# A 4096 x 4096 x 4096 matmul with leaky ReLU in two levels of Winograd's seven products: one more product made of quarters, and the loads of b21 moved behind pieces of a22

## The chip, the cores and the metric

The kernel runs on one core of one Trainium2 chip. The metric is the device time of one execution in microseconds (us), as the median of the runs of a comparison. Before the change it is 1533.41 us, the median of three runs from 1532.85 to 1534.18.

## What is computed

```python
def setup_inputs():
    m, k, n = 4096, 4096, 4096
    return {"a": np.random.randn(m, k).astype(np.float32),
            "b": np.random.randn(k, n).astype(np.float32),
            "alpha": np.float32(0.01)}

def reference(a, b, alpha):
    x = np.matmul(a, b)
    return np.where(x > 0, x, alpha * x)
```

The kernel rounds both matrices to fp16, multiplies with fp32 sums, and applies the leaky ReLU to its fp32 results before they leave.

## The kernel before

**Regions.** The output is cut into 4 groups of 1024 rows (g = 0 to 3) and 4 strips of 1024 columns (j). The first region, (0, 0), is a stage of its own (lines 283 to 440). The other fifteen are made by one loop over `regions` (lines 505 and 506): (0,1), (0,2), (0,3), then (1,2), (1,0), (1,3), (1,1), the same order for g = 2, and (3,2), (3,0), (3,1), (3,3). The names below give a region as (g, j).

**Seven products.** A region is a 2 x 2 block product, made by Winograd's form with seven products in place of eight. `PRODUCTS` (line 653) lists them in their order: a11·b11, a12·b21, s2·b, s3·b, s1·b11', a22·b21', s4·b22', where the s are sums of blocks of A, made once for each group, and the primed blocks of B are sums that VectorE makes in place in every region. One product is 64 matmuls of 128x128 by 128x512 (`product`, line 809 within it). Numbers of products below count from one: the first, ..., the fifth (s1), the sixth (a22), the seventh (s4).

**Quarters.** In some regions the fourth, the sixth or the seventh product is itself made by seven quarter products (`quarter_product`, line 752 within it) of 16 matmuls of 128x128 by 128x256. Such a product has 112 matmuls, of half the width. It needs four more sums of its A block and four of its B block. The sums of A are made by VectorE once for a group (`sums_of_a`) and kept in DRAM (`kept_q`); SyncE loads them again for each region (`load_sums`), 512 KB each. The sums of B are made by VectorE in each region (`t3_of_b` in place, and `sums_of_b` into rooms of a 2 MB tile `t`). All regions with g > 0 other than the last of a group ("turning" regions) make the sixth and the seventh in quarters; all but the first of a group, from g = 1 on, make the fourth in quarters. The fifth is whole everywhere.

**What runs where.** TensorE makes the products in program order. VectorE makes sums, adds PSUM banks onto fp32 results (`add`, line 975; `more`, line 864; line 1133), turns the pieces of A (line 142, a stream transpose) and applies the leaky ReLU (line 313, in `leave`). ScalarE copies PSUM banks and squares data for a check of magnitudes. SyncE (SP) issues most loads and all stores of results; GpSimd (POOL) issues the loads that cast fp32 to fp16: A, and those blocks of B that are not kept. Each engine's queue is in program order. The order is written out by hand (`manual_schedule`), and a framework puts in the waits that buffers and PSUM banks need.

**The turning regions.** In (0,3), (1,1) and (2,1) the next group's A comes in, one 1024 x 1024 quadrant after the other, in four pieces of 512 KB each (`bring_a` = `fetch_a` on GpSimd, `turn_a_in` on VectorE). The last quadrant is a22. At the end of such a region stand, in program order: the loads of the next region's b11 (`fetch_b(i + 1, [(0, 0)], ks)`), the sixth product, then lines 1191 and 1192:

```python
        fetch_b(i + 1, [(1, 0)], (1, 0) if in_quarters else ks)
        bring_a(1, 1, range(3))
        leave(u2_pairs, 1, 0)
```

The first of these loads b21 (two halves of 1 MB, from SP, out of the fp16 copy `kept`), into the buffers that the sixth product reads. The next region's second product reads b21. The fourth piece of a22 comes after; then VectorE makes s1 and s2 of the new group, and in the next region its other sums.

**Other places that the prediction's steps touch.** Line 589 is `b_sum`, a sum of two B blocks. Lines 681, 687, 689 and 691 are the sums of B for quarters (the third, second, fourth and first in that order). Line 735 is in `sums_of_s3`, which makes the sums of s3 into rooms inside a22 and other blocks that are not read at that time; line 701 is in `sums_of_a`. Line 723 loads such a room again from DRAM, and line 770 is a tiny memset that a load of s2 waits for. Three `a16` buffers of 512 KB take the pieces of A and, in other parts, the quarter sums, and the squares of early checks of B (`EARLY`, lines 231 to 264).

Of the kernel before, what the change touches and what calls it, by code (L numbers as in the profile page):

```python
# [8 lines left out]
P = 128  # L9
# [15 lines left out]
KC = 8  # L25
# [6 lines left out]
MT = 4  # L32
# [16 lines left out]
def kernel(  # L49
# [469 lines left out]

    def fetch_unit(i, u, nt):  # L520
        g, j = regions[i]
        half = u // 2
        t = b_pool.tile([P, KC, NT], DT, name="b", tag=f"b{half + 1}{nt + 1}")
        have_b[i, u, nt] = t
        if g > 1 and j == CACHED and (half, nt) == (0, 1):
            move_t("t3", t, u, False)
        elif g and j == CACHED:
            nc.sync.dma_start(t, rows_of(kept[nt], u, 0, KC, True))
        elif half and (g and j == LAST or g > 1 and j in OTHERS):
            nc.sync.dma_start(t.rearrange("p c n -> p (c n)"), kept_half[j][u - 2, nt])  # L530
        else:
            for c in range(0, KC, 4):
                nc.gpsimd.dma_start(t[:, c:c + 4, :], b_rows(j, u, c, 4, nt, g > 0))  # L533
            if j == CACHED:
                wide = KC // (RUNS + [1, 1])[u]
                for c in range(0, KC, wide):
                    nc.sync.dma_start(rows_of(kept[nt], u, c, wide, False), t[:, c:c + wide, :])
# [122 lines left out]
    kept_s2 = dram_pool.tile([2, P, KC * RM], DT, name="kept_s2")  # L660
    kept_q = {name: dram_pool.tile([4, P, QUARTER], DT, name=f"kept_q{name}") for name in ("a22", "s4")}
    kept_s3 = dram_pool.tile([P, QUARTER], DT, name="kept_s3")
# [29 lines left out]

    def sums_of_a(g, name, room):

        x = {key: q.rearrange("p c m e -> p c (m e)") for key, q in quarters_of_a(g, name).items()}
        made = {}

        def make(n, x0, x1, op):
            made[n] = room(n)
            f = lambda t: made[t].rearrange("p (c m) -> p c m", m=2 * HALF) if isinstance(t, int) else x[t]  # L700
# [24 lines left out]
    def sums_of_s3(g, some, room=None):  # L725
# [4 lines left out]
        for n in some:  # L730
# [5 lines left out]
            if n == 4:  # L736
                nc.sync.dma_start(kept_s3, room)

    def s3_rooms(g):
# [43 lines left out]
    for i, (g, j) in enumerate(regions):  # L783
# [66 lines left out]

        def sixth_in_quarters(pairs, banks, v_pairs, v, y, tq, sq):

# [25 lines left out]
            quarter_product(x[0, 1], b[1, 0], into(fourth), True)  # L878
            leave(v_pairs, 1, 1)
            quarter_product(sx(2), t(2), into(one))  # L880
            following(2)
            more(0, 1, one)
            sums_of_b(y7, next_t, (2,))
            more(0, 0, fourth)
            quarter_product(sx(4), b[1, 1], into(other))
            following(1, sq[4])
            next_t[4] = tq[2]
            sums_of_b(y7, next_t, (4,))
            more(0, 1, other)
            quarter_product(sx(3), b[0, 1], into(one))  # L890
            following(3)
            more(1, 0, one)
            more(1, 1, one)
            quarter_product(x[1, 1], t(4), into(third), True)
            more(1, 0, third)
            next_t[1] = tq[4]
            sums_of_b(y7, next_t, (1,))
            return next_t, next_s

# [81 lines left out]

        def leave(pairs, h, nt):
            for r, t in enumerate(pairs):
                leaky(t.rearrange("p m n -> p (m n)"))
                for m in range(2):
# [41 lines left out]
        in_quarters = g > 0 and not turning  # L1027
        in_fourth = in_quarters and not first_of_group
        second_of_group = in_fourth and regions[i - 2][0] != g
        early = [measure(i, *block) for block in EARLY.get((g, j), [])]  # L1030
        for m in early[:1]:
            m.begin()
        if first_of_group and g:
            keep_s2(g)

        product(0, y, True)
# [82 lines left out]
        if late_ones:  # L1119
            late_ones[0].end()  # L1120
        if in_quarters and first_of_group:
            sq = {4: t[:, 3]}
# [4 lines left out]
        if in_fourth or turning and g:  # L1127
            v_pairs, v, parts = fourth_in_quarters(z, tq, {**s3_rooms(g), 4: a_quarter(sx4)})
            if turning:
                for n in range(3):  # L1130
                    turn_a_in(0, 1, n)
            for to, bank in parts:
                nc.vector.tensor_add(to, bank, to)
            if turning:
                add_v()
        else:
            product(3, z, True)
            v_pairs, v = keep(z, side)
        if in_fourth:
            sq = {n: t[:, 3] if n == 4 else new_a16() for n in (1, 2, 3, 4)}  # L1140
# [18 lines left out]
        if final:  # L1159
            judged = judge(b_pool.tile([1, P * 6], FP32, name="line", tag="b12"))  # L1160
            next(judged)
        if in_quarters:
            t3_of_b(quarters_of_b(i, 1, 0))
            sums_of_b(quarters_of_b(i, 1, 0), tq)
            t3_of_b(quarters_of_b(i, 1, 1))
            add_v()
            if final:
                good = next(judged)

        product(4, y, False)  # L1170
        if turning:
            new_s(g + 1, "s1")
        if in_quarters:
            tq, sq = sixth_in_quarters(u2_pairs, [new_bank(zbank + mt) for mt in range(MT)], v_pairs, v, y, tq, sq)
        else:
# [6 lines left out]
        if fifth:  # L1182
            fifth = measure(i + 1, *fifth)
            fifth.begin()
            fifth.end()
        fetch_b(i + 1, [(0, 0)], ks)

        if not in_quarters:
            product(5, z, g > 0)
            add(u2[::-1], z[::-1])  # L1190
        fetch_b(i + 1, [(1, 0)], (1, 0) if in_quarters else ks)
        bring_a(1, 1, range(3))
        leave(u2_pairs, 1, 0)
# [107 lines left out]
```

## Time and profile before

| what | value |
|---|---|
| median of 3 runs | 1533.41 us (1532.85 to 1534.18) |
| the profiled execution | 1537.09 us |
| its span, first to last instruction | 1535.2 us |
| TensorE busy | 1523.4 us, 8667 matmuls |
| VectorE busy | 1158.9 us, 1207 instructions |
| ScalarE busy | 425.5 us |
| granted TensorE clock, mean | 1.00 |
| moved by DMA | 351.26 MB, mean 229 GB/s |

The span is the time between the first and the last instruction of the profiled execution; what lies around it (1.9 us here) is not profiled. In the profile, idle time of an engine is put down to what ended it. A busy TensorE is counted from the start of a matmul to its modelled end, so a matmul's mean of 379 ns (128x512) is longer than the distance from one to the next, and lengths of products are better read from the distance of their starts.

Where the regions that matter begin, from the starts of their first matmuls: (0,3) 315.45 us, (1,2) 412.14, (1,0) 506.38, (2,2) 785.88, (2,0) 879.40, (2,3) 971.45, (2,1) 1063.38, (3,2) 1159.87, each with its products in the order above.

### The profile page before, as it was taken

What the parts mean: (1) busy time and instruction counts of PE and PEld (TensorE: products, weight loads), DVE (VectorE), ACT (ScalarE), POOL (GpSimd) and SP (SyncE); (2) the same over time, 40 slices, a digit from 0 to 9 for tenths busy, and PEclk for the clock granted to TensorE, in tenths of its full rate; (3) what the DMA queues carried; (4) which work ended last, traced back from release to release, by engine and by line L of the source; (5) the groups of instructions that cost most, each with busy time, mean ns of one, the idle gap of its engine ahead of it and who ended that gap; (6) DMA issues with size and microseconds to landing.
All of it is one profiled execution on the core that took longest, in us unless ns stands there. A gap on an engine that the chain in (4) does not pass through costs nothing. (4 is left out here: it accounts for less than half of the span.)

```text
span 1535.2 us, 21782 instructions
## 1 busy us (share of the span) xinstructions
PE 1523.4 (99%) x8667; PEld 846.8 (55%) x8667; DVE 1158.9 (75%) x1207; ACT 425.5 (28%) x730; POOL 258.3 (17%) x426
## 2 busy tenths in 40 slices
PE   9999999999999999999999999999999999999998
PEld 4444444444446567574544747557554475746656
DVE  4368867766699686768769798676987978687677
ACT  2201344646310213103551130312464103041210
POOL 5641110243202011022220001010331100101000
PEclk9999999999999999999999999999999999999999
DMA  9999895998879999899798939669899892949824
GB/s 246 183 212 209 232 280 174 177 195 177 223 284 280 252 288 272 249 288 259 168 284 272 319 147 207 268 154 323 168 228 298 230 345 75 292 160 193 306 97 140
DMA packets 192002, 351.26 MB, mean 229 GB/s; under 512 B 18705, under 2 KB 131601, under 8 KB 178834
## 3 DMA queue, kind: packets, MB, share of 16 engines
q0 software_dynamic: 119808, 112.22, 46.4%
q1 hardware_dynamic: 65458, 211.98, 37.1%
q10 hardware_dynamic: 6624, 25.56, 4.4%
q8 instruction: 70, 1.15, 0.3%
q14 instruction: 42, 0.34, 0.1%
HBM read 344.98 MB, written 114.82 MB: 300 GB/s over the span
## 5 line engine op out<-in xcount | busy, mean ns | idle before, releaser
L809 PE MATMUL ps<-b,a 128*128 128x512 f16 x2624 | 570.6, 379 | 0.0
L809 PE MATMUL ps<-b,s 128*128 128x512 f16 x2240 | 489.2, 379 | 0.4 <-DVE b L589 0.4
L809 PEld LDWEIGHTS <-a 128*128 128x128 f16 x2624 | 256.8, 98 | 307.6
L809 PEld LDWEIGHTS <-s 128*128 128x128 f16 x2240 | 219.1, 98 | 263.1 <-issue 1.2
L589 DVE TENSOR_TENSOR b<-b 128x4096 f16<-128x4096 f16 x104 | 234.7, 2287 | 47.1 <-DMA b<-in_b_dram 37.7
L533 POOL DMA_DIRECT2D b<-in_b_dram x128 | 94.9, 746 | 861.0 <-PE ps L752 436.8
L822 ACT COPY c<-ps 128x512 f32<-128x512 f32 x164 | 84.8, 596 | 468.1 <-PE ps L809 424.5
L142 DVE STREAM_TRANSPOSE a<-a 128x512 uint32<-128x512 uint32 (+2 forms) x120 | 127.2, 1108 | 100.8 <-DMA a<-in_a_dram 100.7
L133 POOL DMA_DIRECT2D a<-in_a_dram x252 | 137.5, 553 | 266.1 <-ACT junk L608 88.2
L752 PEld LDWEIGHTS <-q 128*128 128x128 f16 x1424 | 139.3, 98 | 16.8 <-issue 0.7
L608 ACT ACTIVATE junk<-a 128x512 bf16<-128x512 f16 x192 | 121.1, 631 | 98.6 <-DMA a<-in_a_dram 93.2
L313 DVE SCALAR_TENSOR_TENSOR c<-c 128x1024 f32<-128x1024 f32 (+2 forms) x123 | 141.7, 1194 | 3.4 <-ACT c L822 3.2
L231 ACT ACTIVATE sq<-b 128x2048 bf16<-128x2048 f16 x64 | 118.4, 1910 | 38.7 <-DVE sq L240 30.9
L975 DVE TENSOR_TENSOR c<-ps,c 128x512 f32<-128x512 f32 x140 | 87.5, 682 | 55.0 <-PE ps L809 41.7
L752 PEld LDWEIGHTS <-a 128*128 128x128 f16 x1200 | 117.4, 98 | 19.0 <-issue 1.4
L283 PE MATMUL ps<-b,a 128*128 128x512 f16 x512 | 112.5, 379 | 1.6 <-DVE a L142 1.0
L752 PE MATMUL ps<-b,q 128*128 128x256 f16 x784 | 92.0, 273 | 0.6 <-DVE c L864 0.6
L752 PE MATMUL ps<-b,a 128*128 128x256 f16 x752 | 88.3, 273 | 0.0
L283 PEld LDWEIGHTS <-a 128*128 128x128 f16 x512 | 49.6, 98 | 62.4 <-issue 1.8
L911 ACT COPY c<-ps 128x512 f32<-128x512 f32 x9 | 5.3, 587 | 269.8 <-DMA out_dram<-c 118.9
L752 PEld LDWEIGHTS <-s 128*128 128x128 f16 x624 | 61.1, 98 | 7.1
L864 DVE TENSOR_TENSOR c<-ps,c 128x512 f32<-128x512 f32 x80 | 52.3, 687 | 14.3 <-PE ps L752 14.3
(104 smaller groups left out, 904.1 us busy)
## 6 DMA issues: line engine op xcount, KB each, us to landing
b<-in_b_dram POOLq DMA_DIRECT2D x136, 512.0 KB, 11.7
out_dram<-c SPq DMA_DIRECT2D x240, 256.0 KB, 6.4
a<-in_a_dram POOLq DMA_DIRECT2D x244, 128.0 KB, 5.7
b<-kept_half SPq DMA_DIRECT2D x28, 1024.0 KB, 11.1
b<-kept SPq DMA_DIRECT2D x20, 1024.0 KB, 9.2
q<-kept_qs ACTq DMA_DIRECT2D x40, 512.0 KB, 7.7
s<-kept_s SPq DMA_DIRECT2D x18, 1024.0 KB, 7.7
q<-kept_qa SPq DMA_DIRECT2D x28, 512.0 KB, 7.8
```

Source lines behind the costliest of these rows:

```text
L133: nc.gpsimd.dma_start(a16[32 * q:32 * q + 32], src.rearrange("(g i) w -> i g w", i=32))
L142: nc.vector.transpose(part.rearrange("p c m e -> p c (m e)").bitcast(U32) .rearrange("p c (g i) -> p g c i", i=32), src[:, :, i * n:(i + 1 ...
L231: nc.scalar.activation(to, self.parts[n], SQUARE)
L283: nc.tensor.matmul(ps, a_cols(at[0, h, u], c, mt, (h, u) == (0, 0)), bt[0, u, nt][:, c, :], start=first, stop=last,)
L313: nc.vector.scalar_tensor_tensor(t, t, alpha, t, op0=MULT, op1=MAX if alpha <= 1 else MIN)
L533: nc.gpsimd.dma_start(t[:, c:c + 4, :], b_rows(j, u, c, 4, nt, g > 0))
L589: nc.vector.tensor_tensor(f(to), f(x0), f(x1), op)
L608: nc.scalar.activation(junk, piece[:, q, :], SQUARE, accum_out=to[:, 4 * n + q:4 * n + q + 1])
L752: nc.tensor.matmul(to[m], xq[:, c // 2, rows, c % 2], yq[:, c, :], start=first and c == 0 and m < banks, stop=c == KC - 1, skip_group_chec ...
L809: nc.tensor.matmul(banks[mt], a_cols(t, c, mt, t is first_a), B(half, nt, k)[:, c, :], start=first and (k, c) == todo[0], stop=(k, c) == t ...
L822: nc.scalar.copy(kept[mt], banks[mt])
L975: nc.vector.tensor_add(to, bank, to)
```

## The change

It does two things.

**b21 behind a22.** In turning regions, b21's first half is loaded after the second piece of a22 is turned, and its second half after the third. A memset of one column on VectorE stands before each load and writes its buffer, so that the load, on SP, waits for VectorE to come to it. The halves come in the order 0, 1.

**The fifth in quarters in (2,3).** A new function makes it. For it, (2,0) makes the four sums of s1 and keeps them in DRAM, and (2,3) loads them. Its partial sums go from PSUM by ScalarE into rooms in a22 (where a sum of s3 lay), and from there VectorE adds them onto the banks `y`. So that sum of s3 is kept in DRAM too (in (2,2)), and loaded again at the start of (2,1). The sums of B for the sixth, which were made during the fifth, are now made between the steps of the fifth and the sixth, and the sums of A for the sixth are loaded after those of the fifth.

```diff
-    def fetch_unit(i, u, nt):
+    def fetch_unit(i, u, nt, later=False):
         t = b_pool.tile([P, KC, NT], DT, name="b", tag=f"b{half + 1}{nt + 1}")
         have_b[i, u, nt] = t
+        if later:
+            nc.vector.memset(t[:, :1, :1], 0.0)
...
+    FIFTH = {(2, 3)}
+    kept_s31 = dram_pool.tile([P, QUARTER], DT, name="kept_s31")
...
             nc.vector.tensor_tensor(sx[n], x0, x1, op)
             if n == 4:
                 nc.sync.dma_start(kept_s3, room)
+            if n == 1 and g in [of for of, _ in FIFTH]:
+                nc.sync.dma_start(by_chunk(kept_s31), sx[1])
...
+        def fifth_in_quarters(y, one, other, tq, sq, between):
+            b = quarters_of_b(i, 0, 0)
+            x = quarters_of_a(g, "s1")
+            t = lambda n: b_quarter(tq[n])
+            sx = lambda n: a_quarter(sq[n])
+            onto = lambda r, n: [y[2 * r + m][:, n * HALF:(n + 1) * HALF] for m in range(2)]
+            rooms = by_chunk(x21(g, "a22")).bitcast(FP32)
+            rooms = [rooms[:, :2], rooms[:, 2:]]
+            def copied(bank):
+                rooms.append(rooms.pop(0))
+                nc.scalar.copy(rooms[1], pair(bank))
+                return rooms[1]
+            def more(r, n, room):
+                for m, to in enumerate(onto(r, n)):
+                    nc.vector.tensor_add(to, to, room[:, m])
+            quarter_product(x[0, 0], b[0, 0], into(one), True)
+            room = copied(one)
+            quarter_product(sx(4), b[1, 1], onto(0, 1))
+            more(0, 0, room)
+            next(between)
+            quarter_product(x[1, 1], t(4), onto(1, 0))
+            quarter_product(sx(2), t(2), into(one))
+            room = copied(one)
+            quarter_product(x[0, 1], b[1, 0], onto(0, 0))
+            more(0, 1, room)
+            next(between)
+            quarter_product(sx(1), t(1), into(other), True)
+            room = copied(other)
+            more(0, 1, room)
+            more(1, 1, room)
+            quarter_product(sx(3), b[0, 1], into(one))
+            room = copied(one)
+            for m in range(2):
+                to = pair(y[2 + m])
+                nc.vector.tensor_add(to, to, room[:, m].unsqueeze(1).to_broadcast([P, 2, HALF]))
...
-            leave(v_pairs, 1, 1)
+            if between:
+                next(between)
+            else:
+                leave(v_pairs, 1, 1)
             quarter_product(sx(2), t(2), into(one))
             following(2)
             more(0, 1, one)
+            if between:
+                t3_of_b(y7)
             sums_of_b(y7, next_t, (2,))
             more(0, 0, fourth)
+            if between:
+                leave(v_pairs, 1, 1, (0,))
...
             sums_of_b(y7, next_t, (1,))
+            if between:
+                leave(v_pairs, 1, 1, (1,))
...
+        if i and regions[i - 1] in FIFTH:
+            for c in range(KC // 2):
+                nc.sync.dma_start(by_chunk(x21(g, "a22"))[:, c], by_chunk(kept_s31)[:, c])
         product(0, y, True)
...
+        s1_sums = {}
+        if s1_here:
+            sums_of_a(g, "s1", lambda n: t[:, n - 1], (1, 2, 3), s1_sums)
+        if in_fifth:
+            t5 = {2: t[:, 0], 4: t[:, 1], 1: t[:, 2]}
+            t3_of_b(quarters_of_b(i, 0, 0))
+            sums_of_b(quarters_of_b(i, 0, 0), t5, (2, 4))
...
-            for to, bank in parts:
+            for n, (to, bank) in enumerate(parts):
+                if in_fifth and n == 2:
+                    sums_of_b(quarters_of_b(i, 0, 0), t5, (1,))
                 nc.vector.tensor_add(to, bank, to)
-            if turning:
+            if turning or in_fifth:
                 add_v()
...
-        if in_fourth:
+        if s1_here:
+            sums_of_a(g, "s1", lambda n: t[:, 3], (4,), s1_sums)
+        if in_fifth:
+            s5 = {n: t[:, 3] if n == 3 else new_a16() for n in (4, 2, 1, 3)}
+            load_sums("s1", s5, (4, 2, 1, 3))
+        elif in_fourth:
...
+        if in_fifth:
+            fifth_in_quarters(y, new_bank(zbank + 3), new_bank(zbank + 1), t5, s5, between)
+            sq = {n: t[:, 3] if n == 3 else new_a16() for n in (1, 2, 4, 3)}
+            load_sums("a22", sq, (1, 2, 4, 3))
...
-        fetch_b(i + 1, [(1, 0)], (1, 0) if in_quarters else ks)
-        bring_a(1, 1, range(3))
+        if turning:
+            bring_a(1, 1, [0, 1])
+            fetch_unit(i + 1, 2, 0, True)
+            bring_a(1, 1, [2])
+            fetch_unit(i + 1, 3, 0, True)
+        else:
+            fetch_b(i + 1, [(1, 0)], (1, 0) if in_quarters else ks)
         leave(u2_pairs, 1, 0)
```

`for_the_sixth` is the generator that `between` stands for: it makes the sums of B for the sixth in three steps, one at each `next`. In the sixth of (2,3) the rooms and banks are taken in another order, so that none waits for the fifth's last steps.

## Prediction

> **What bounds the kernel now.** I read the page's head first, then TensorE's waits, then the chain of waits in order of time, and then VectorE's timeline ahead of each wait found.
>
> ```profile
> PE 1523.4 (99%) x8667; PEld 846.8 (55%) x8667; DVE 1158.9 (75%) x1207; ACT 425.5 (28%) x730; POOL 258.3 (17%) x426
> ...
> PE ps L752 <- DVE q L689: 1.2, 1, 1.2
> ...
> PE ps L752 <- DVE c L864: 0.6, 1, 0.6
> PE ps L809 <- DVE b L589: 0.4, 1, 0.4
> ```
>
> TensorE is busy for 99% of the span at clock 1.00. Only three waits lie after the first region. So there are two ways to gain: fewer columns through TensorE, and these three waits. From the starts of the matmuls around them they cost more than the rows' idle time: (1,2)'s sixth takes 12.95 us instead of 12.23 (0.73 lost), (1,0)'s second product 14.34 instead of 13.81 (0.53), (2,1)'s fourth 13.61 instead of 12.23 (1.39). The chain prices a product:
>
> ```profile
> 1107.17 1.24 DVE q L687
> 1108.40 0.02 issue
> 1108.42 1.24 DVE q L689
> 1109.66 0.04 issue
> 1109.70 8.89 PE ps L752 x80
> ...
> 1295.00 12.23 PE ps L752 x112
> 1307.22 13.81 PE ps L809 x64
> ```
>
> A product in quarters takes 12.23 us, a whole one 13.81. Everything after 1109.70 is TensorE without a gap, so whatever is won or lost by then reaches the end undiminished. Next, VectorE where A comes in at the end of (0,3), and in (1,0):
>
> ```profile
> 409.91 2.11 DVE L142 STREAM_TRANSPOSE a<-a 128x512 uint32<-128x512 uint32 x2 [8.89 <-DMA a<-in_a_dram]
> ...
> 489.92 0.69 DVE L864 TENSOR_TENSOR c<-ps,c 128x512 f32<-128x512 f32 x1
> ...
> 529.71 2.29 DVE L589 TENSOR_TENSOR b<-b 128x4096 f16<-128x4096 f16 x1 [8.86 <-DMA b<-in_b_dram]
> ...
> 534.77 4.62 DVE L589 TENSOR_TENSOR b<-b 128x4096 f16<-128x4096 f16 x2 [0.39 <-DMA b<-in_b_dram]
> ```
>
> VectorE sits idle for 8.89 us until a22's first piece is there. From then to 463 us it has nearly no idle time, and at 489.92 it gives a bank free 0.73 us late: it carries its lateness from the turn. The wait in (1,0) comes from loads of b: from 461 to 535 us the DMA engines are full in each slice (mean share 1.13), and the 16 loads of b there take a median of 24.4 us. The third place is (2,1):
>
> ```profile
> 1018.00:1046.00 28.00, 28.00 (x196) 18.98 (x195) 20.36 (x22) 1.76 (x3) 5.91 (x8) 1.00 1.10 220
> 1046.00:1074.00 28.00, 28.00 (x211) 20.41 (x210) 19.06 (x23) 9.84 (x9) 0.00 (x0) 1.00 1.00 373
> 1074.00:1078.00 4.00, 4.00 (x20) 1.82 (x19) 3.81 (x8) 1.62 (x4) 2.54 (x5) 1.00 0.49 97
> 1078.00:1093.00 15.00, 15.00 (x72) 6.77 (x70) 12.01 (x10) 5.68 (x16) 6.12 (x12) 1.00 1.06 194
> ...
> 1090.38 2.11 DVE L142 STREAM_TRANSPOSE a<-a 128x512 uint32<-128x512 uint32 x2 [2.49 <-DMA a<-in_a_dram]
> 1092.82 2.10 DVE L142 STREAM_TRANSPOSE a<-a 128x512 uint32<-128x512 uint32 x2 [0.33 <-DMA a<-in_a_dram]
> ```
>
> The last two columns of the windows are DMA share and GB/s: full from 1018 to 1074, half idle for 4 us, full again. VectorE waits for pieces of A until 1092.82 and then works without a gap to the sum (L689) that TensorE takes at 1109.70. So (2,1)'s wait is one of arriving data.
>
> **The change part by part.** *b21 behind a22, at (0,3).* b11 and b21 (4 MB) now stand ahead of the pieces; 2 MB of it go behind. The transfers from 391 to 410 run at the rate of 1 MB in about 3.3 us, so the pieces come some 6 us earlier, and with them VectorE's sums for (1,2). A few of these will then meet other limits (b22 lands at about 427, where VectorE takes it at 432.34 now), so I count 5 us. That is more than 0.73: the wait in (1,2) goes, -0.73. VectorE's stores (kept_s, kept_q) go out 5 us sooner too, partly into DMA time that is idle around 452, ahead of the full stretch of 461 to 535; its end, the last b22, then moves from 534.7 to some time between 530 and 534.7. The wait there is 0.53, and TensorE comes there 0.73 earlier, so the wait goes if that end moves by 1.3 us or more, of some 4.5 possible: -0.53. Sum -1.26; bounds 0 and -1.26. On the other side stands b21 itself: first half issued at about 407, second at 410, and the 1 MB loads of this kind land in a median of 9.2 us (12.4 us where pieces come beside them), so at 419 to 422; the second product takes it at 425.95 and 432.9. Covered by 7 us. VectorE's memsets are of 0.06 us (the one on L770), and their buffers are free by then: the sixth product ends at 398.3. Queued behind the waiting load on SP are only u2's stores, which VectorE makes ready later still; queued behind the memsets on VectorE is the third piece, which isn't there yet. At (1,1) and (2,1) the same move gains nothing, since (2,2) and (3,2) have no wait.
>
> *The fifth in quarters.* 13.81 - 12.23 = -1.58. Its start waits for VectorE: after the sums of B at 1020.83 it now makes three sums for quarters (1.25, 1.25, 1.14) before it frees bank `fourth` (0.69), at 1025.2 against a start at 1025.11: +0.1. Then come two adds, one sum (1.14), three adds, `add_v` (2.35) and the first adds of 128x256 onto `y`. No row has an add from PSUM to PSUM; the nearest, L940, takes 0.43 into SBUF, so 0.9 for two, done at 1031.8. TensorE needs them at 1032.2: 0.4 in hand. At twice the price it would wait 0.5; below nothing it can't cost. The rest of VectorE's work fits into its 3.68 us of idle time ahead of 1038.48 and, spread, into the sixth.
>
> *Loads of sums in (2,3).* The four for the fifth go where those for the sixth went, issued 1018.3 to 1023.6, the last landed by 1032.8, needed at 1035.6. Those for the sixth now go when buffers come free, at 1028.7, 1032.2, 1035.7 and 1037.4, and are needed at 1039.2, 1042.7, 1044.4 and 1046.2. Rows for such loads here: median 8.9 us on SP, 7.4 to 10.4 on ACT's queue 10 us later. So the margins are 1.6, 1.6, -0.2 and -0.1: I take +0.3 of new wait, bounds 0 and 1.7.
>
> The Trainium skill bears on this: DMA: Bandwidth & Descriptors (Queues, rings and completion order) says each DMA engine takes turns between queues by packet. From 1018.5 to 1046 SP's queue moved 2.10 MB in 576 packets and GpSimd's 4.05 MB in 4071, 3.6 KB and 1.0 KB each; by that rule the sums would win over b's loads and come without a wait, which makes 1531.2. But the loads of 1018 to 1024 took 8.9 us all the same, so the sum goes by the row.
>
> *Sums of s1 in (2,0).* Four on VectorE, 4 x 1.22 = 4.9 us, beside idle time of 3.68 + 1.11 + 0.69 there. Their rooms in `t` are wanted again: VectorE must wait until the stores (issued at about 932 to 934.3) have landed. Stores of this kind took 6.6 to 7.4 us in (1,2) at equal load, so 942: VectorE goes on with the sum that TensorE wants at 948.7 ready at 945. SP's loads for the sixth wait behind the fourth store, issued at about 938.4 instead of 926.4; the last needs that store landed (946), lands at 953.5 and is needed at 954. I take +0.2, bounds 0 and 3.5 (landings of 13.3 us, as kept_half's stores).
>
> *(2,1).* The fifth brings 2 MB more, and the kept s3 sum 0.5 MB: at 373 GB/s 6.7 us of DMA inside the full stretch. Against it are 2 us idle after 1074, and pieces that GpSimd can issue 1.5 us sooner, as TensorE is earlier. With s2's 1 MB load standing amid the pieces in either case, I expect them about 1.2 us sooner on the clock where TensorE is 1.5 us sooner, so the wait grows by 0.3: +0.3. Bounds: -1.39 (wait gone) and 6.7 - 2.0 = 4.7 later on the clock, which is +6.2 against a TensorE that is 1.5 earlier.
>
> Sum: -1.26 - 1.58 + 0.1 + 0.3 + 0.2 + 0.3 = -1.94. The profiled execution took 1537.09 (span 1535.2), 3.7 above the median; I take the sum off the median: 1533.41 - 1.94 = **1531.5 us**.
>
> **The rivals.** (A) *Pieces of (2,1) late, slower than before.* The backlog of 6.7 us is met by only 2 us of idle DMA, so the last piece lands 4.7 us later, the chain to L689 shifts whole, and the fifth's gain drowns in the wait: -1.26 + 4.7 = +3.4, 1536.9. For it: shares of 1.00 to 1.10 over 56 us. Against it: most of the extra bytes come early, and GpSimd's loads of b11 and b12, landed by 1052.5 and used from 1063 on, can give way. It decides from a landing 1.3 us later on.
>
> (B) *The wait of (2,1) goes as well.* Pieces come with TensorE's earlier start and v's stores, now split and later, leave room: -1.26 - 1.58 + 0.1 - 1.39 = -4.1, 1529.3. Against it: nothing in the change brings these pieces forward.
>
> (C) *b21's move doesn't do what it says*: VectorE's lead is lost to waits for stores of sums (it has such waits of 0.5 to 0.8 at 463 to 474), and both waits of group 1 stay: -0.68, 1532.7. For it: the DMA engines are full there. Against: 5 us of lead for 0.73.
>
> (D) *(2,0) waits for its stores*: +3.5 in place of 0.2: 1534.8. For it: b's loads beside them take 10.5 us. Against: 6.6 to 7.4 for the same stores.
>
> **How the numbers follow.** Forecast 0.52, A 0.08, B 0.17, C 0.12, D 0.11. The forecast's own spread is 1530.3 to 1533. Less than 0.2% (3.07 us: below 1530.34, above 1536.48) I take as about what a measurement can't tell from no change. Faster: B and 0.03 of the forecast, 0.20. Slower: A and 0.02 of D, 0.10. Same: 0.70. The range 1529.4 to 1534.9 leaves out A and about half of B.
>
> **What would show it.** Right: no wait on L864 in (1,2) and none on L589 in (1,0); VectorE's idle time at the end of (0,3) down from 8.89 to about 3; the fifth of (2,3) in 12.2 to 12.5 us; a wait of 1 to 3.5 us on L689's successor in (2,1). Wrong: TensorE waiting in (2,0)'s sixth for a sum or its load, more than 1 us in (2,3)'s sixth, a second product in (1,2), (2,2) or (3,2) that waits for b21, or (2,1)'s fourth above 16 us.

## The result, and the profile after

The changed kernel takes 1537.74 us, the median of 11 executions from 1534.06 to 1543.66. The kernel before, in the same comparison, takes 1534.02 (11 executions, 1532.54 to 1536.68). The ratio is 1.0024, 95% interval 1.0014 to 1.0034: 3.72 us slower, just over the 3.07 us below which the prediction takes two times as the same. The forecast was 1531.5, the range 1529.4 to 1534.9; the result lies outside it.

The profiled execution of after took 1537.21 us (span 1534.3), that of before 1537.09 (span 1535.2). So the two profiles end together, though the medians are 3.7 apart. That has to be understood first, and it is done by cutting a profile into the stretch from the start of region (0,1) to the modelled end of the last matmul, which holds everything that was changed, and the rest, which holds the first region and what lies around the span:

| profile | execution us | (0,1) starts | stretch us | rest us |
|---|---|---|---|---|
| before | 1537.09 | 122.06 | 1407.30 | 129.79 |
| after | 1537.21 | 120.57 | 1408.58 | 128.63 |
| after, five more executions | 1537.12, 1535.69, 1535.95, 1534.90, 1536.39 | 120.69 to 121.32 | 1407.59, 1406.65, 1406.24, 1405.48, 1407.24 | 129.04 to 129.71 |
| s31_alone (below): nothing in the stretch waits | 1532.31 | 120.51 | 1404.66 | 127.65 |

The rest is 127.65 to 130.77 us in the twenty profiles of this study. In the six profiles of kernels whose fifth is whole it is 128.42 on average, in the six of after 129.25. Before's median of 1534.02 less 128.42 is 1405.6, so the usual execution of before loses some 0.9 us to waits in the stretch (at most 1.7, by the smallest rest), where its profile lost 2.65. This is an estimate, since before was profiled once, and that profile was taken on an execution above all eleven others. After's median less 129.25 is 1408.5. So of the 3.7 us between the medians some 2.9 lie in the stretch and some 0.8 outside it.

The part outside can be seen without a profile too, since the span of every execution is on record. What lies around the span is 1.87 to 2.17 us in all 106 executions of before that the experiments were compared with, and 1.96 to 3.07 us in the eleven of after, with a median of 2.93. Behind the span the trace has no instruction of the program, but it has loads of instructions (8 KB each): one in before's profile, which ends 2.1 us behind the span, and two in after's, the second ending 3.2 us behind it. That this second load takes the time is likely and not shown. The prediction has no term for it.

TensorE's waits after (the line, what it waited for, us in total, times, longest):

```profile
PE ps L762 <- DVE q L694: 2.8, 1, 2.8
...
PE ps L762 <- ACT c L977: 1.1, 1, 1.1
PE ps L819 <- DMA b<-in_b_dram: 0.8, 1, 0.8
```

L762, L819, L694 and L592 are L752, L809, L689 and L589 of before. The two waits of group 1 are gone, and of the three above, two are new. The lengths of the products, from one start to the next, where they are not the full 13.81 (whole) or 12.23 us (quarters) in each profile ((2,0)'s second product, 13.93, and the last product of all, 12.39, are left out, being the same in before):

| product | before | after | five more executions of after |
|---|---|---|---|
| (1,2) sixth | 12.95 | 12.23 | 12.23 each |
| (1,0) second | 14.34 | 13.81 | 13.81 each |
| (2,0) sixth | 12.23 | 12.36 | 13.22, 12.56, 12.41, 13.12, 13.22 |
| (2,3) first | 13.81 | 14.79 | 13.81 each |
| (2,3) fourth | 12.23 | 12.47 | 12.46 or 12.47 |
| (2,3) fifth | 13.81 | 12.22 | 12.22 each |
| (2,3) seventh | 12.23 | 13.45 | 13.47, 13.41, 13.43, 13.47, 13.47 |
| (2,1) fourth | 13.61 | 15.17 | 14.27, 14.06, 13.78, 12.28, 13.92 |

After's column against before's sums to +1.29, which is the difference of the two stretches (1.28): nothing is lost anywhere else. Now the places in turn.

*b21 behind a22.* VectorE at the end of (0,3) (start, us, line, operation, and in brackets the idle time and what ended it):

```profile
401.46 2.10 DVE L142 STREAM_TRANSPOSE a<-a 128x512 uint32<-128x512 uint32 x2 [1.94 <-DMA a<-in_a_dram]
404.19 2.11 DVE L142 STREAM_TRANSPOSE a<-a 128x512 uint32<-128x512 uint32 x2 [0.63 <-DMA a<-in_a_dram]
```

The idle time of 8.89 us ahead of a22 is 1.94 now, and the first piece is turned 8.5 us sooner (7.0 sooner counted from the start of (0,1)).

*The fifth.* VectorE's adds from SBUF onto PSUM, which no row of before had, and the seventh's place on ScalarE:

```profile
1029.38 0.76 DVE L881 TENSOR_TENSOR ps<-ps,a 128x256 f32<-128x256 f32 x2
...
1032.62 0.76 DVE L881 TENSOR_TENSOR ps<-ps,a 128x256 f32<-128x256 f32 x2 [1.35 <-PE ps L762]
...
1046.74 1.22 DVE L313 SCALAR_TENSOR_TENSOR c<-c 128x1024 f32<-128x1024 f32 x1
```
```profile
1055.75 0.59 ACT L977 COPY c<-ps 128x512 f32<-128x512 f32 x1 [18.97 <-DMA out_dram<-c]
```

A pair of adds takes 0.76, overlap included, and VectorE is there 1.35 us ahead of TensorE for the second pair. But v's first pair of output blocks now gets its leaky ReLU only at 1046.74 (L313), its stores are issued at 1047.98, and the seventh's first copy (L977) needs one of those `c` buffers: it waits for the store until 1055.75, and TensorE waits for the copy. Before, v left as a whole, earlier in the sixth.

*(2,1).* VectorE where the pieces of A come in, and the chain behind it:

```profile
1084.08 2.11 DVE L142 STREAM_TRANSPOSE a<-a 128x512 uint32<-128x512 uint32 x2
1090.05 2.10 DVE L142 STREAM_TRANSPOSE a<-a 128x512 uint32<-128x512 uint32 x2 [3.86 <-DMA a<-in_a_dram]
1092.62 2.11 DVE L142 STREAM_TRANSPOSE a<-a 128x512 uint32<-128x512 uint32 x2 [0.47 <-DMA a<-in_a_dram]
```
```profile
1108.22 1.24 DVE q L694
1109.46 0.04 issue
1109.50 8.89 PE ps L762 x80
```

The last sum comes at 1109.46 where it came at 1109.66; counted from the start of (0,1) that is 1.29 us later, while TensorE wants it 0.27 sooner (its start in the fourth, 1103.06 against 1104.82 by the same count). The DMA engines in the windows shown of before (the last two columns: DMA share, GB/s):

```profile
1046.00:1074.00 28.00, 26.94 (x192) 18.57 (x190) 21.39 (x27) 10.64 (x10) 0.55 (x1) 1.00 1.06 366
1074.00:1078.00 4.00, 4.00 (x20) 1.79 (x19) 3.89 (x7) 1.07 (x2) 3.75 (x7) 1.00 1.09 308
```

The 4 us that were half idle (share 0.49) are full now (1.09). The execution moves 356.50 MB in place of 351.26: the sums of s1 are stored and loaded (4.2 MB), the kept s3 sum too (1.0 MB). Who pays is seen in the landings from 1013 to 1046, first before, then after:

```profile
b<-in_b_dram POOLq DMA_DIRECT2D x8, 512.0 KB, 9.9
q<-kept_qa SPq DMA_DIRECT2D x4, 512.0 KB, 8.9
```
```profile
b<-in_b_dram POOLq DMA_DIRECT2D x8, 512.0 KB, 13.0
q<-kept_qs SPq DMA_DIRECT2D x4, 512.0 KB, 7.7
q<-kept_qa SPq DMA_DIRECT2D x4, 512.0 KB, 6.5
```

There are twice the loads of sums on SP, and both groups land sooner, in the median, than the one did before; GpSimd's casting loads go from 9.9 to 13.0 us. The pieces of A in (2,1) are GpSimd's loads too: the first of them took 2.8 us from its issue to its landing before (issued at 1074.46), and takes 6.4 us after (issued at 1072.69). The rule of the Trainium skill that the prediction weighed (DMA: Bandwidth & Descriptors, Queues, rings and completion order: turns by packet) agrees with this pair of rows.

### The profile page after: what moved, and what is told of

The parts are those of the page before. It is cut to its first block, busy times and chain, and to the rows that moved or that the text cites. A ratio compares the mean times of both kernels' runs of the same rounds, so it can differ in the third digit from the quotient of the medians.

```text
span 1534.3 us, 21931 instructions
## 1 busy us (share of the span) xinstructions
PE 1522.1 (99%) x8715; PEld 851.6 (56%) x8715; DVE 1172.4 (76%) x1231; ACT 428.2 (28%) x734; POOL 258.8 (17%) x426
## 2 busy tenths in 40 slices
DMA packets 194258, 356.50 MB, mean 232 GB/s; under 512 B 18913, under 2 KB 132833, under 8 KB 181090
## 5 line engine op out<-in xcount | busy, mean ns | idle before, releaser
L819 PE MATMUL ps<-b,a 128*128 128x512 f16 x2624 | 570.7, 379 | 0.8 <-DMA b<-in_b_dram 0.8
L819 PE MATMUL ps<-b,s 128*128 128x512 f16 x2176 | 475.2, 379 | 0.0
L819 PEld LDWEIGHTS <-a 128*128 128x128 f16 x2624 | 256.7, 98 | 308.7 <-issue 1.1
L819 PEld LDWEIGHTS <-s 128*128 128x128 f16 x2176 | 212.9, 98 | 255.2 <-issue 0.4
L592 DVE TENSOR_TENSOR b<-b 128x4096 f16<-128x4096 f16 x104 | 234.7, 2286 | 45.6 <-DMA b<-in_b_dram 30.7
L762 PEld LDWEIGHTS <-q 128*128 128x128 f16 x1488 | 145.5, 98 | 18.3 <-issue 1.2
L313 DVE SCALAR_TENSOR_TENSOR c<-c 128x1024 f32<-128x1024 f32 (+2 forms) x123 | 141.8, 1192 | 3.7 <-ACT c L832 3.5
L762 PEld LDWEIGHTS <-a 128*128 128x128 f16 x1200 | 117.4, 98 | 20.4 <-issue 3.0
L1041 DVE TENSOR_TENSOR c<-ps,c 128x512 f32<-128x512 f32 x140 | 87.6, 683 | 44.7 <-PE ps L819 33.5
L762 PE MATMUL ps<-b,q 128*128 128x256 f16 x816 | 95.6, 273 | 0.0
L762 PE MATMUL ps<-b,a 128*128 128x256 f16 x752 | 88.3, 273 | 0.0
L977 ACT COPY c<-ps 128x512 f32<-128x512 f32 x9 | 5.3, 586 | 256.9 <-PE ps L762 122.9
L762 PEld LDWEIGHTS <-s 128*128 128x128 f16 x672 | 65.8, 98 | 7.8 <-issue 0.2
L762 PE MATMUL ps<-q,q 128*128 128x256 f16 x528 | 62.9, 273 | 1.1 <-ACT c L977 1.1
```

What stands on the lines that cost most here:

```text
L313: nc.vector.scalar_tensor_tensor(t, t, alpha, t, op0=MULT, op1=MAX if alpha <= 1 else MIN)
L592: nc.vector.tensor_tensor(f(to), f(x0), f(x1), op)
L762: nc.tensor.matmul(to[m], xq[:, c // 2, rows, c % 2], yq[:, c, :], start=first and c == 0 and m < banks, stop=c == KC - 1, skip_group_chec ...
L819: nc.tensor.matmul(banks[mt], a_cols(t, c, mt, t is first_a), B(half, nt, k)[:, c, :], start=first and (k, c) == todo[0], stop=(k, c) == t ...
```

## The experiments

Theory: the fifth's bytes, in a stretch where the DMA engines are full, make transfers behind them land late (pieces of A, stores that free `c` buffers, loads of sums). Rivals: the fifth's own order of work on VectorE and ScalarE loses the time; or b21's loads, or the one load of the kept s3 sum, block a queue at a bad place. Diffs are against the changed kernel. Ratios are against before on the same chip.

**The parts alone.** b21_alone makes no fifth in quarters, fifth_alone has lines 1191 and 1192 as they were, fifth_31 makes the fifth in quarters in (3,1), where no A comes in behind it.

```diff
-    FIFTH = {(2, 3)}
+    FIFTH = set()
```

> The fifth stays whole everywhere; only the loads of b21 are moved. Late pieces (the 5 MB that the fifth adds to the transfers of group 2 delay the pieces of A in (2,1), and its fourth product waits): 1.3 us faster than before, (1,2)'s sixth at 12.23 us and (1,0)'s second product at 13.81, (2,1)'s fourth at 13.6 as before, and runs within 4 us of each other. Costly turn (b21's move is what slows the kernel, by loads that come late in some executions): 3 to 5 us slower, with runs spread over 8 us or more.

```diff
-        if turning:
-            bring_a(1, 1, [0, 1])
...
+        fetch_b(i + 1, [(1, 0)], (1, 0) if in_quarters else ks)
+        bring_a(1, 1, range(3))
```

> The fifth of (2,3) in quarters, with b21 loaded ahead of a22 as before. Late pieces: slower than the changed kernel by the 1.3 us that b21's move is worth, so about 5 us slower than before, with (2,1)'s fourth at 15 us or more. Costly turn: 1.6 us faster than before, less about 0.5.

```diff
-    FIFTH = {(2, 3)}
+    FIFTH = {(3, 1)}
```

> The same fifth in quarters, with b21's move, but in (3,1), with the sums of s1 of group 3 made in (3,0); no A comes in afterwards. Late pieces: the gain of 1.6 us comes through, less waits of 0 to 2.4 us in (3,1) and (3,3): 0.5 to 2.9 us faster than before. Order of the fifth (the new waits in its own region, for c buffers above all, make the loss): no faster than b21's move alone by more than 0.5 us, waits as in (2,3): 1 us in the next region's or its own first product, 1.2 us in the seventh.

Measured: b21_alone 1533.46 against 1534.33, ratio 1.0000 [0.9991, 1.0008], where a gain of 1.3 us or a loss of 3 to 5 was expected; both waits of group 1 are gone from its profile. fifth_alone 1535.95, 1.0021 [1.0007, 1.0035], with (1,0)'s second product at 14.50 and (2,3)'s seventh at 13.49. Neither theory expected that: without b21's move the kernel is no slower than with it (1.0024). In this profile, whose group 1 is as in before, (1,2)'s sixth takes its full 12.23, so the wait there doesn't stand in every execution without the move. fifth_31 1536.72, 1.0022 [1.0013, 1.0032]. So the fifth loses the time and b21's move doesn't; but b21's move does not clearly win any either. If bytes ahead of A were all, fifth_31 would be free of the loss, and it isn't. In its profile (2,1) is at its full 12.23, the fourth of (3,1) takes 12.98, and its seventh 16.10: a wait for L977's `c` buffer as in (2,3), and half a clock behind it. The columns are window, its length, busy time of PE, PEld, DVE, ACT, POOL, then granted clock, DMA share, GB/s:

```profile
1427.00:1429.00 2.00, 0.55 (x6) 0.34 (x4) 1.24 (x2) 0.04 (x1) 0.00 (x0) 1.00 1.20 251
1429.00:1433.00 4.00, 3.40 (x17) 2.46 (x17) 0.00 (x0) 0.55 (x1) 0.00 (x0) 0.58 1.07 415
```

TensorE stands still for 2.21 us from 1427.4, then 16 matmuls start 213 ns apart in place of 109: 1.7 us more. The wait is of the same form as the one in (2,3), and v leaves late here too. So the rival of the fifth's own order holds for a part of the loss, as leave_early shows below for (2,3).

**Bytes without the fifth.** s31_late only moves the load of the kept s3 sum, from the start of (2,1) to just ahead of its fourth product. The others have b21's move and the fifth whole: s31_alone keeps only that store and load of 0.5 MB; four_more and eight_more add to it four or eight stores of 512 KB to DRAM in (2,3), whose data nobody reads; four_more_again is four_more once more.

```diff
-        if i and regions[i - 1] in FIFTH:
-            for c in range(KC // 2):
-                nc.sync.dma_start(by_chunk(x21(g, "a22"))[:, c], by_chunk(kept_s31)[:, c])
         product(0, y, True)
...
             nc.sync.dma_start(sx4, kept_s3)
+        if i and regions[i - 1] in FIFTH:
+            for c in range(KC // 2):
+                nc.sync.dma_start(by_chunk(x21(g, "a22"))[:, c], by_chunk(kept_s31)[:, c])
```

> The changed kernel, with the kept sum of s3 loaded again ahead of (2,1)'s fourth product instead of at its start, so 0.5 MB less beside the pieces of A. Late pieces: the third piece lands 1 to 1.5 us earlier and the time falls by as much against the changed kernel, to 2 to 2.7 us slower than before. Costly turn and order of the fifth: as the changed kernel, 3.7 us slower than before.

```diff
-    FIFTH = {(2, 3)}
+    FIFTH = set()
+    S31 = {(2, 3)}
...
-        if i and regions[i - 1] in FIFTH:
+        if i and regions[i - 1] in S31:
```

> b21's move, and of the fifth nothing but the 0.5 MB kept in (2,2) and loaded again at the start of (2,1); the fifth stays whole. If that load alone takes the pieces' time (it stands ahead of them by itself): 1.5 to 3 us slower than b21's move alone, (2,1)'s fourth at 14 to 15.5 us, with runs above 1537. If it costs only on top of the fifth's other 4 MB (a backlog that reaches into (2,1)): within 0.6 us of b21's move alone.

four_more and four_more_again, with this besides:

```diff
             load_sums("a22", sq, (1, 2, 3, 4))
+            if (g, j) in S31:
+                for n in range(4):
+                    nc.sync.dma_start(by_chunk(kept_q["s1"][n]), by_chunk(x21(g, "a22")))
```

> b21's move and the kept sum of s3 loaded again, the fifth whole, and four stores of 512 KB more from SP in (2,3), whose data nobody reads: the fifth's bytes without its order. Bytes alone: (2,1)'s fourth at 14 us or more, 1.5 to 4 us slower than b21's move alone, with runs above 1537. Blocked queue: within 0.8 us of b21's move alone, (2,1)'s fourth below 13.3.

> The same kernel as four_more, for another profile. Bytes: if this execution is slower than 1537, the difference to the first profile (1534.10) stands in (2,1)'s fourth alone, at first as wait and, above some 4 us, as half clock behind it. Rival: it stands in several places.

eight_more goes over `[0, 1, 2, 3] * 2` there.

> As the kernel with four more stores of 512 KB, but eight (4 MB). Bytes: the backlog grows by another 2 MB, 5 us at 373 GB/s, so (2,1)'s fourth waits 3 us or more longer than with four; a wait that long brings the half clock, seen in the profile as matmuls of 128x256 at 213 ns instead of 109 right behind it; median 1540 to 1545, lowest above 1536. Rival (the time lost doesn't grow with bytes, it comes from the chance order of packets): median within 1 us of 1537.7, and no half clock.

| kernel | median us | range | ratio |
|---|---|---|---|
| s31_late | 1535.04 | 1533.75 to 1536.81 | 1.0007 [0.9998, 1.0016] |
| s31_alone | 1532.95 | 1532.31 to 1534.06 | 0.9993 [0.9984, 1.0002] |
| four_more | 1537.69 | 1534.10 to 1544.67 | 1.0023 [1.0007, 1.0038] |
| four_more_again | 1537.27 (one execution) | | |
| eight_more | 1543.03 | 1541.14 to 1545.17 | 1.0052 [1.0032, 1.0072] |

Four stores of 2 MB in all, with no fifth and no extra VectorE work, lose 3.3 us against before, about as much as after does and with as wide a spread; eight lose 8.7. That four come so near to after's loss is partly chance: by the medians of the spans four_more loses all of its 3.3 us inside the span (1535.7 against 1532.4), and the changed kernel, timed again as after_again, 2.2 inside (1534.3 against 1532.1) and 1.0 outside. The 0.5 MB alone cost nothing: they count only on top of the others, where loading them some 35 us later (from 1103.53 on in place of 1068.76) gives some 2.5 us back by the ratios (s31_late, 1.0007 in place of 1.0023 and 1.0024). VectorE at the pieces in (2,1), in s31_alone and then in four_more_again, whose (0,1) starts within 0.1 us of each other:

```profile
1086.03 4.29 DVE L142 STREAM_TRANSPOSE a<-a 128x512 uint32<-128x512 uint32 x4 [0.95 <-DMA a<-in_a_dram]
```
```profile
1091.32 4.26 DVE L142 STREAM_TRANSPOSE a<-a 128x512 uint32<-128x512 uint32 x4 [4.01 <-DMA a<-in_a_dram]
```

The same two pieces are turned 5.3 us later. Of that, 2.2 us are TensorE's own lateness: (2,1) starts at 1062.78 in place of 1060.58, and GpSimd issues the first load of A 11.1 us after that start in both. The other 3.1 are landing time: this load took 4.1 us in the one and 7.8 in the other. The fourth product takes 12.23 in the one and 14.86 in the other. In four_more_again the seventh of (2,3) takes 1.33 us too long as well, waiting for a `c` buffer, although v leaves there as in before: late stores alone do that too. (The added stores also stand ahead of v's in SP's queue, so for this wait their bytes and their place in the queue aren't told apart; the pieces of A are on GpSimd's queue.) Against four_more's first profile the stretch is 3.28 us longer, in three places and not in (2,1)'s fourth alone, as the theory of bytes expected: 1.16 there, 1.33 in this seventh, and 0.79 in (1,0)'s second product, which lies ahead of the added stores and can't come from them. In eight_more, all of it stands in the seventh, and none in (2,1)'s fourth, where it was expected (L763 and L978 are L762 and L977 of after):

```profile
PE ps L763 <- ACT c L978: 7.1, 1, 7.1
```
```profile
1053.00:1060.00 7.00, 2.63 (x25) 2.20 (x23) 0.00 (x0) 0.00 (x0) 0.00 (x0) 0.91 1.10 357
1060.00:1063.00 3.00, 0.30 (x2) 0.24 (x2) 0.00 (x0) 0.59 (x1) 0.00 (x0) 0.50 1.06 395
1063.00:1066.00 3.00, 3.00 (x18) 2.12 (x17) 0.00 (x0) 0.00 (x0) 0.00 (x0) 0.57 1.04 416
```

TensorE waits 7.1 us for the stores, then runs at a granted clock of 0.50 to 0.57 for 3 us; (2,1) behind it has no wait left: its first load of A, issued 11.1 us after the region's start as elsewhere, landed in 5.6 us. That the transfers ahead of it were worked off while TensorE stood still is likely and not shown.

**Repairing the waits one by one.** leave_early is s31_late with v's first pair leaving ahead of the fourth sum of B. all_three adds to it the fourth sum for the fifth one add later, and in (2,0) three loads for the sixth ahead of s1's fourth store. mended has, for that last part, the rooms of the third and fourth sums of a22 exchanged, so that the load behind the store is wanted last.

```diff
-            if between:
-                next(between)
-            else:
-                leave(v_pairs, 1, 1)
+            leave(v_pairs, 1, 1, (0,) if between else (0, 1))
...
+                next(between)
                 t3_of_b(y7)
...
-            if between:
-                leave(v_pairs, 1, 1, (0,))
```

> As the kernel with the sum of s3 loaded late, and v's first pair leaves ahead of the sum of B for the sixth's last quarter product, instead of behind five steps. If (2,3)'s seventh waits for v's stores to free a c buffer: the first store goes out 5 us sooner, the seventh takes 12.23 instead of 13.43, and the time falls by 1.2 us against the kernel with the late load. If the wait is of another kind (ScalarE held up by something else): no change.

all_three, in (2,0):

```diff
         if s1_here:
+            sq = {n: new_a16() for n in (1, 2, 3)}
+            load_sums("a22", sq, (1, 2, 3))
             sums_of_a(g, "s1", lambda n: t[:, 3], (4,), s1_sums)
+            sq[4] = t[:, 3]
+            load_sums("a22", sq, (4,))
```

> As the one with v's first pair early, and two more moves: the fourth sum of B for the fifth is made behind the add that frees the fifth's first bank (the 0.24 us at its start), and (2,0) issues three of the sixth's loads ahead of the store of s1's fourth sum (0.13 to 0.9 us there). Theory of waits one by one: all of (2,3) at 12.23 us a product in quarters and (2,0)'s sixth at 12.23; 1.4 to 1.6 us below b21's move alone, 2.3 to 2.9 below before. Rival (whatever is won in (2,3) is lost again in the wait of (2,1), since its pieces do not come sooner): (2,1)'s fourth longer by as much, no faster than b21's move alone.

mended, in its place:

```diff
+        elif s1_here:
+            sq = {n: t[:, 3] if n == 3 else new_a16() for n in (1, 2, 4, 3)}
+            load_sums("a22", sq, (1, 2, 4, 3))
```

> The kernel with the late load and v's first pair early; the fourth sum of B for the fifth behind the add that frees its first bank; and in (2,0) the rooms of the third and the fourth sum of a22 exchanged, so that the load that waits for s1's last store is the one needed 1.75 us later. Waits one by one: (2,3)'s fourth 12.23, (2,0)'s sixth 12.23 to 12.4, and 1.0 to 1.6 us below b21's move alone, that is 2.0 to 2.6 below before. Wait moved on: (2,1)'s fourth takes it over, at b21's move alone.

Measured: leave_early 1534.20 (1533.59 to 1535.85), 1.0003 [0.9994, 1.0012], and the seventh is at 12.23: the late leave was the cause of that wait. By the time alone it isn't clear of s31_late, whose interval it overlaps. all_three missed: 1540.88, 1.0043 [1.0029, 1.0056], with a new wait in (2,0)'s sixth, and half a clock behind it:

```profile
964.09 1.28 PE L762 MATMUL ps<-b,q 128*128 128x256 f16 x9 [3.94 <-DMA q<-kept_qa]
```

The fourth store stood behind three loads in SP's queue, and the load that needs its room behind it. mended is without that: 1533.87 (1532.03 to 1537.32), 0.9999 [0.9986, 1.0012]; every product of (2,0) and (2,3) has its full speed, and one wait is left:

```profile
PE ps L762 <- DVE q L694: 0.8, 1, 0.8
```

So with these repairs the change costs nothing any more, and it doesn't win clearly either, where 2.0 to 2.6 us were expected: the pieces of A in (2,1) remain late (its fourth takes 13.19). By the medians of the spans mended is 1.1 us faster than before (1531.3 against 1532.4), and most of that is lost again outside the span (2.8 us against 2.0).

**b21 ahead of v's stores.** The kept loads of b21 in (2,3) stand behind v's second pair of stores on SP, and b's loads could block what follows. b21_sooner lets that pair leave behind them; mended_sooner does it on top of mended.

```diff
             sums_of_b(y7, next_t, (1,))
-            if between:
-                leave(v_pairs, 1, 1, (1,))
...
+        if in_fifth:
+            leave(v_pairs, 1, 1, (1,))
         leave(u2_pairs, 1, 0)
```

> The changed kernel, with one order on SP's queue undone: at the end of (2,3) the loads of the next region's b21 go ahead of the stores of v's second pair, as they stood ahead of its due time before, instead of behind them. Blocked queue (b21's loads wait 8 us behind stores that VectorE makes ready late, and then bunch with b22, s2, the stores and the sum of s3 ahead of the pieces): 1.5 to 2.5 us faster than the changed kernel, (2,1)'s fourth at 13 to 14 us, few runs above 1538. Bytes alone (the 5 MB more): no change, 1537.

> The kernel before this one in the list, and b21's loads ahead of v's second stores. Blocked queue: (2,1)'s fourth at 12.23 to 12.6, 0.3 to 0.8 us faster than the kernel before it. Bytes alone: the same as it. Late stores of v as a new wait (c buffers of the seventh's second pair): a wait of up to 1 us in (2,3)'s seventh.

Measured: 1537.64, 1.0019 [1.0005, 1.0032], and 1536.54, 1.0015 [1.0002, 1.0028]. Neither gains; the first product of (2,1) now waits for a `c` buffer and is 1.3 us and 1.8 us too long. (2,1)'s fourth takes 14.27 and 12.93, against 12.28 to 15.17 in after and 13.19 in mended, so nothing speaks for the blocked queue as the cause.

**The changed kernel again.** Nothing is edited in these five.

> The changed kernel unchanged, beside the others on one chip. All theories: 2 to 4 us slower than before, with runs up to 8 us apart. If this profile falls on a slower execution than the first one, the theory of late pieces expects (2,1)'s fourth above 15.2 us, and a half clock behind that wait or behind the one in (2,3)'s seventh.

> The changed kernel, for another profile. Bytes: (2,1)'s fourth at 14 to 18 us; where the clock's mean is 0.998 or less, a half clock behind its wait or behind the one in (2,3)'s seventh. Rival: (2,1)'s fourth below 14 and the time lost elsewhere.

> The changed kernel again, one profiled execution, to see where an execution above 1539 us loses its time. If the long waits are followed by half a clock: an execution above 1539 us shows a wait of TensorE of 2.5 us or more in group 2, with some 16 matmuls of 128x256 behind it at 213 ns in place of 109, 1.4 to 2 us more than the wait itself. If instead the time goes in more waits at full clock: products of (2,0), (2,3) and (2,1) add up to the difference, and no stretch behind a wait shows a granted clock near 0.5. An execution below 1538 us should show neither, as the three so far.

> The same, for the same end: half a clock behind a wait of 2.5 us or more if the execution is above 1539 us, none if it is below 1538 us; or, by the other reading, more waits at full clock.

> The same, for the same end: half a clock behind a wait of 2.5 us or more if the execution is above 1539 us, none if it is below 1538 us; or, by the other reading, more waits at full clock.

after_again, timed as well: 1537.12, 1.0023 [1.0014, 1.0032], so the result repeats. The products of the five are in the table of the result. The last three were meant for an execution above 1539 us and took 1535.95, 1534.90 and 1536.39, so where such an execution loses its time was not seen. What is known of such executions is their clock: of after's eleven, the five above 1539 us show a mean of 0.997 or 0.998, the six below 0.999 or 1.000. Before has such executions too, but fewer: 3 of 106 are above 1539 us, against 5 of 11 and, in after_again, 4 of 11.

## Why the prediction was wrong

**The kinds of work were right.** The fifth takes 12.22 us (-1.59, forecast -1.58). Its first adds onto PSUM take 0.76 a pair (forecast 0.9, with 0.4 in hand; 1.35 was in hand for the second pair). The waits on L864 and L589 went in all six profiles of after (among the other kernels with b21's move, four_more_again has the one in (1,0) again), and b21 was covered: no second product of (1,2), (2,2) or (3,2) waits for it. VectorE's idle time at the turn went from 8.89 to 1.94 ahead of the first piece (forecast about 3).

**The base was wrong.** The step "I take the sum off the median" set waits of one profile, taken 3.7 us above the median, against the median. The -1.26 of b21's move was there to win in that execution; the usual execution of before had some 0.9 us of waits in all (worked out above). The runs agree: with b21's move alone the ratio is 1.0000 [0.9991, 1.0008], in s31_alone, which has the move too, 0.9993 [0.9984, 1.0002], and in fifth_alone one of the two waits of group 1 is absent without the move. The stretch of before's profile is 1407.30, that of its median about 1405.6, so this step alone is worth some 1.7 us, at least 0.9.

**Terms of the sum.** The start of the fifth's wait: +0.23 to +0.24 in each profile, forecast 0.1. Loads of sums in (2,3): none, forecast 0.3; the row of 8.9 us was too dear, they landed in 6.5 to 7.7. Sums of s1 in (2,0): +0.13 to +0.99, mean 0.59, forecast 0.2; there the step's own margin of half a microsecond was the right thing to fear. (2,1): +0.3 against before's profile, and the six profiles give a wait of 1.68 on average against 1.39, so +0.29; but against b21_alone and s31_alone, where the fourth takes 12.77 and 12.23, it is 1.1 to 1.7. Four stores of as many bytes as the fifth has there, with no fifth, bring it to 13.70 and 14.86 in the two profiles of four_more.

**The terms that were missing.** +1.18 to +1.24 in (2,3)'s seventh, in every profile. The change part by part counted the split `leave` of v nowhere, except in rival B as something that would leave room. It holds two `c` buffers 6 us longer, and the seventh's first copy is the next to want one. leave_early takes it away and the wait with it. The other missing term is the 0.8 us outside the span.

Together the terms measured in the six profiles are -1.26 - 1.59 + 0.24 + 0.59 + 0.16 (b11 late in one of six) + 1.23 + 0.29 = -0.34 against before's profile, in place of -1.94: 1.6 us of the miss. The stretch of the six is 1406.96 on average, 1.4 above the usual before of about 1405.6; that of after's median is some 1408.5, so another 1.5 us lie in executions that no profile caught. With 1.7 for the base and 0.8 outside the span, these make up the 5.7 us between the forecast -1.94 and the measured +3.72, as far as the average rests hold.

**The rivals.** A was right in kind for a part of the loss, with a chance of 0.08: the backlog is met by the 4 us of half idle DMA (now at 1.09), the pieces come 1.3 us later by (0,1)'s start, and the chain to L694 shifts whole. Its size, 4.7, was not reached in any profile of after, nor by the 3.1 us of landing time between s31_alone and four_more_again; that its time, 1536.9, is near the result is luck, since the other terms are in the result too. Its counter-argument, that GpSimd's loads can give way, was the wrong way round: they do give way, and the pieces of A are among them. C is right that the -1.26 isn't won, but not in why: the waits went, and the median hardly moved. D's place was right and its price too high. B falls.

**What stays open.** What the 0.8 us outside the span are, and where after's executions above 1539 us lose their time. Half a clock behind a long wait is what fifth_31, eight_more and all_three show, and a mean clock lower by 0.001 over 1534 us is 1.5 us, about one such stretch; for after itself that is argued, not shown. Also open is a wait of 5.4 us in (1,2) in the profile of all_three, the highest of its six executions (1547.52). It stands ahead of all that all_three's own edits touch.

## What to carry to other kernels

Before a gain is counted on a wait of one profile, ask where that execution lies among the others: a wait that only a late execution has is not in the median. Where the DMA engines are full, price added bytes at the consumer whose transfer lands last with the least slack, and look first at the queue that gives way, here GpSimd's casting loads. When a store is moved later, find the next writer of its buffer: it costs there and not where the store stands. Where a change makes the program longer, compare the spans as well as the times.

## What was not expected of the hardware

A wait of TensorE can cost more than its length. After waits of 2.2 us (fifth_31), 4.1 (all_three) and 7.2 (eight_more) 13 to 16 matmuls of 128x256 started 213 ns apart, about 3 us in all, at a granted clock of 0.50 to 0.58, which adds 1.4 to 1.7 us, and after one of 5.4 us, in (1,2) of all_three, the clock was 0.50 for some 4 us, which added 2.2. After waits of 2.0 and 2.9 us in (2,1), in two profiles of after, it stayed at 1.00. The Trainium skill (TensorE: Matmul & The Clock Gate, Part 1: The HAM clock gate) says that the clock falls to half after an idle window of about 3.4 us and needs a busy one to come back, with windows that run free of the program. The length of the slow stretch agrees; a wait of 2.2 us is shorter than the page's window, and there the measurement decides.

Extra loads of 512 KB on SP's queue did not slow each other (median 8.9 us before, 6.5 and 7.7 with twice as many in the same 33 us), while GpSimd's went from 9.9 to 13.0 beside them.
